# Gate and up side by side for the last 256 feed-forward columns, one group for token numbers and gates, selection sums on TensorE: a diffusion block with expert-choice routing on one core

## The chip, the cores and the metric

The kernel runs on one core of one Trainium2 chip. A core has TensorE (PE in the profile; its weight loads are a line of their own, PEld), VectorE (DVE), ScalarE (ACT), GpSimd (POOL) and SyncE (SP), which here issues most of the transfers. The metric is the time of one execution on the device in microseconds (us); lower is better. The kernel before has a median of 1981.69 us over three runs (1981.35 to 1982.66).

## The reference

One layer over 1024 latent tokens of 1024 numbers and 256 context tokens: a modulated RMSNorm, a token mixer (a Fourier group and a recurrent group), a gated residual, and then the part that this change touches, a mixture of 16 experts in which each expert chooses its 128 tokens. At the end stands a last RMSNorm.

```
def expert_choice_ffn(h, w_router, w_gate, w_up, w_down):
    cap = EC_CAPACITY * n // N_EXPERTS                      # 128 of 1024 tokens
    aff = softmax(h @ w_router)                             # 16 experts
    g, idx = lax.top_k(swapaxes(aff, 1, 2), cap)            # each expert picks its tokens
    xg = h[bidx, idx]
    hid = silu(xg @ w_gate) * (xg @ w_up)                   # 1024 -> 2816 columns
    y = (hid @ w_down) * g[..., None]                       # 2816 -> 1024
    return zeros_like(h).at[bidx, idx].add(y)
```

All of it is float32. An expert has 3 x 1024 x 2816 weights, so the 16 experts read 553.6 MB.

## The kernel before

**The stream of weights.** `make_stream` lists the weights of all experts in halves of 1 MB (128 partitions by 2048 float32). An expert has six groups of hidden columns, five of 512 and a last one of 256. A group of 512 has four gate and up halves (gate, gate, up, up) and two halves of `w_down`; the last group has two halves from one array `wt`, the first with its gate columns and the second with its up columns, and one half of `w_down`. That makes 33 halves an expert, 528 in all. The down halves of a group come behind the gate and up halves of the next one.

**One half.** SyncE loads it into one of ten buffers (`raw`). ScalarE rounds it to the matmul's 32-bit format (`hi`, line 227), VectorE subtracts (`lo`, line 228), into one of four pairs of buffers. TensorE then multiplies three times for each product (`mm3`, line 611): high by high, high by low, low by high. In `moe`, at step m, the order written out by hand is: the matmuls of half m, the activation if a group ended, the rounding of half m + 4, the load of half m + 10, and then whatever `plan` has put at this step. TensorE, ScalarE and VectorE follow this order exactly; a wait of one instruction holds up what is behind it on its engine.

**A group.** `half` (lines 1592 to 1614) puts the gate product of a group into one half of a PSUM tile `gu` and the up product into the other, each in a bank of its own; for the last group the matmuls are 256 columns wide and there are 24 in each half of the stream, for the other groups 512 wide and 12. `act` (line 1616) takes the silu of gate on ScalarE and multiplies by up on VectorE (`hid`). `hid_t` (line 1623) transposes the result on TensorE and splits it again (`hh`, `hl`) for the down product `y`; for the first two experts it stands two steps behind the group's end, for the others one.

**The selection.** In the course of expert 0 and the first half of expert 1, `topk_a`, `topk_p` and `topk_b` find each expert's threshold in 15 rounds, two bits at a time, one round every three steps; each round has six small operations on VectorE and eight matmuls. The first two experts' tokens are already known from the phase before. `gates` (line 1364), at step 3, cuts the routing weights into three bfloat16 parts (`aux`). `topk_end` (line 1399) turns the threshold into slots: masks `m` of the tokens above and at the threshold, for 8 blocks of 128 tokens and 16 experts; the number of such tokens ahead of each token, from a triangular matmul inside a block (line 1410) and from the totals of the blocks (line 1411), which VectorE adds up block by block (`off`, line 1419); then the slot numbers `slT`, partly on VectorE and partly on GpSimd. `plan` puts its four pieces at steps 45, 48, 48 and 49.

**The pick.** `prep` (line 1456) makes a one-hot tile `oh` from the slots on VectorE, multiplies it on TensorE with the token numbers `tokb` (eight matmuls of 2 columns, line 1466) and with the three parts of the gates (eight of 3 columns, line 1468), reduces both on VectorE, and has GpSimd gather the rows. For expert 2 the one-hot tile stands at step 51 and the matmuls at step 54, behind the transposes of expert 1's fourth group.

**Memory.** On the left lie the constants, then a pad of 32 float32 per partition, the ten `raw` buffers and three pairs of `hi` and `lo`; on the right the rest of the expert phase.

Of the kernel before, what the change touches and what calls it, by code (L numbers as in the profile page):

```python
# [99 lines left out]
def lay_out(inp):  # L100
# [22 lines left out]
    for gi, nm in ((0, "lru_wa"), (1, "lru_wi")):  # L123
# [12 lines left out]
        [wg[..., 2560:].transpose(0, 2, 1, 3), wu[..., 2560:].transpose(0, 2, 1, 3)], 2  # L136
# [25 lines left out]
class Kern:  # L162
    HP, HT, LATE = 50, 300, -100
    PAD = 32
# [1199 lines left out]
    def gates(self):  # L1364
        self.aux = self.mo.tile([128, 8, E, 3], BF16, name="aux")
        self.triple(self.aux, self.mo.tile([128, 8, E], F32, name="r1"), self.lg)
# [32 lines left out]
    def topk_end(self):  # L1399
# [9 lines left out]
        mf = m.rearrange("p a b e -> p (a b e)")  # L1409
        nc.tensor.matmul(p[:, 0:256], self.utri, mf, start=True, stop=True)  # L1410
        nc.tensor.matmul(p[:, 256:512], self.ones2, mf, start=True, stop=True)
        yield
        q = S("pre", [2, 8, E])
        V.tensor_copy(q.rearrange("p a b e -> p (a b e)"), p[:, 0:256])
        tot = p[:, 256:512].rearrange("p (a b e) -> p a b e", a=2, b=8)
        off = S("off", [2, 9, E])
        G.memset(off[:, :, 0], 0.0)
        for b in range(8):
            V.tensor_tensor(off[:, :, b + 1], off[:, :, b], tot[:, :, b], op=ALU.add)
        G.tensor_tensor(q, q, off[:, :, 0:8], op=ALU.add)  # L1420
        need = S("need", [E])
        G.tensor_scalar(need, off[:, 0, 8], -1.0, float(CAP), op0=ALU.mult, op1=ALU.add)
        nb = need[:, None].to_broadcast([128, 8, E])
        yield
        sel, sl = S("sel", [8, E]), S("sl", [8, E])
        V.tensor_tensor(sel, q[:, 1], nb, op=ALU.is_lt)
        G.tensor_tensor(sel, sel, m[:, 1], op=ALU.mult)
        G.tensor_tensor(sel, sel, m[:, 0], op=ALU.add)
        V.tensor_tensor(sl, q[:, 1], nb, op=ALU.min)
        G.tensor_tensor(sl, sl, q[:, 0], op=ALU.add)  # L1430
        G.tensor_scalar(sl, sl, 1.0, None, op0=ALU.add)
        self.slT = S("slT", [8, E])
        G.tensor_tensor(self.slT, sl, sel, op=ALU.mult)
# [22 lines left out]
    def prep(self, e):  # L1456
# [8 lines left out]
        for b in range(8):  # L1465
            self.nc.tensor.matmul(p[:, 0:2], oh[:, b], self.tokb[:, b], start=b == 0, stop=b == 7)
        for b in range(8):
            self.nc.tensor.matmul(p[:, 2:5], oh[:, b], self.aux[:, b, e], start=b == 0, stop=b == 7)
# [33 lines left out]
    def make_stream(self):  # L1502
# [3 lines left out]
        def gu(e, j):  # L1506
            self.at[e, j] = len(self.S)
            if j < 5:
                for g, n in ((0, "wg"), (1, "wu")):
                    for h in range(2):  # L1510
                        self.S.append(("g", e, j, g, h, a[n][e, j][:, 2048 * h:2048 * h + 2048]))
            else:
                for g in range(2):
                    self.S.append(("g", e, j, g, 0, a["wt"][e][:, 2048 * g:2048 * g + 2048]))
            self.end[e, j] = len(self.S) - 1
# [76 lines left out]
    def half(self, m):  # L1592
        _, e, j, g, h, _ = self.S[m]
        hi, lo = self.hls.pop(m)
        if self.S[m][0] == "g":
# [4 lines left out]
            w = 512 if j < 5 else 256  # L1600
            nk = 2048 // w
            for i in range(nk):
                k, s = nk * h + i, slice(w * i, w * i + w)
                self.mm3(p[:, g, 0:w], xh[:, k], xl[:, k], hi[:, s], lo[:, s], k == 0, k == KD - 1)
# [11 lines left out]
    def act(self, e, j):  # L1616
        nc = self.nc
        w, p = 512 if j < 5 else 256, self.gu.pop((e, j))
        hid = self.hid[e, j] = self.mo.tile([128, 512], F32, tag="hid", name=f"hid{e}{j}", bufs=2)
        nc.scalar.activation(hid[:, 0:w], p[:, 0, 0:w], AF.Silu)  # L1620
        nc.vector.tensor_tensor(hid[:, 0:w], hid[:, 0:w], p[:, 1, 0:w], op=ALU.mult)  # L1621
# [102 lines left out]
    def plan(self):  # L1724
# [31 lines left out]
        steps((m, m + 3, m + 3, m + 4), tail)  # L1756
        at(m + 4, lambda: next(tail, None))
# [79 lines left out]
```

## Time and profile before

| | |
|---|---|
| median of 3 runs | 1981.69 us (1981.35 to 1982.66) |
| profiled execution | 1983.2 us, its span 1981.4 us |
| busy of the span | TensorE 1899.9 us (96%), VectorE 1750.4 (88%), ScalarE 1357.3 (69%), GpSimd 137.0 (7%) |
| mean granted TensorE clock | 0.980 |
| HBM traffic | 622.98 MB read, 26.74 MB written |
| chain that ended last | TensorE 76%, VectorE 9%, DMA 6% |

The phase before the experts takes the first 430 us; the experts run from there to the end, one each 94.3 us in the regular part. The span runs from the first to the last instruction on the core; the profiled execution's time holds what lies around it too. In a timeline each row is an instruction (or several of one kind, xN): when it started, how long it is shown, and in brackets how long its engine was idle before it and what ended that. A matmul's shown length includes its way through the array, so several overlap; the pace is read from start to start. Notation such as `gu<-hi,xgh` gives the tile written and the tiles read. The granted clock is a share of 2.4 GHz.

### The profile page before, as it was taken

The page shows a single profiled execution, that of the slowest core. Times are in us where ns is not written, and L with a number is a line of the kernel's source. Part 1 is how long each engine was busy: PE and PEld are TensorE (multiplying, and loading weights), DVE is VectorE, ACT ScalarE, POOL GpSimd, SP SyncE. Part 2 cuts the span into 40 slices and gives each one's busy share as a digit, 9 for nine tenths or more (in the row PEclk, how much of TensorE's full clock was granted, in tenths as well). Part 3 has the DMA queues.
Part 4 walks back from the last instruction along what each step waited for, and adds up shares of the span by engine and source line. Part 5 has one row for each costly group of instructions (what it writes and reads, how often), then busy time and mean ns, then how long its engine had stood idle before and what let it go on. Part 6 is the DMA issues. An engine that isn't in the chain of part 4 may idle for free.

```text
span 1981.4 us, 24505 instructions
## 1 busy us (share of the span) xinstructions
PE 1899.9 (96%) x9434; PEld 1559.9 (79%) x9434; DVE 1750.4 (88%) x1629; ACT 1357.3 (69%) x1094; POOL 137.0 (7%) x134
## 2 busy tenths in 40 slices
PE   7989889969999999999999999999999999999996
PEld 2777777857787888888888888888888888888885
DVE  7889787789998989898999999998989898989897
ACT  6567643346676777777777777777777777777775
POOL 2310101220002000000000000000000000000000
PEclk9999989979999999999999999999999999999998
DMA  8353554578999999999999999999999999999994
GB/s 330 112 159 123 191 173 149 207 285 334 350 357 339 379 368 390 381 386 367 388 363 391 355 406 364 396 366 381 379 381 375 384 381 376 385 375 387 366 390 178
DMA packets 113956, 651.34 MB, mean 329 GB/s; under 512 B 12743, under 2 KB 20472, under 8 KB 46254
## 3 DMA queue, kind: packets, MB, share of 16 engines
q1 hardware_dynamic: 100718, 602.55, 79.2%
q0 software_dynamic: 10816, 38.82, 6.9%
q10 hardware_dynamic: 2304, 8.39, 1.1%
q8 instruction: 74, 1.21, 0.2%
q14 instruction: 44, 0.36, 0.0%
HBM read 622.98 MB, written 26.74 MB: 328 GB/s over the span
## 4 chain that ended last, share of the span: by engine, by line
PE 76%; DVE 9%; DMA 6%; issue 5%; ACT 1%; POOL 1%; SPq 0%; POOLq 0%; DVEq 0%; ACTq 0%
PE gu L611 44%; PE y L611 22%; PE mx L611 4%; DVE lo L228 3%; DMA mraw<-in_wmod_dram 3%; PE ht L1627 2%; DMA x<-in_x_dram 1%; DVE macc L839 1%; PE xt L1498 1%; ACT hi L227 1%; DMA trr<-in_trig_dram 1%; PE hp L1185 1%; PE pq L611 1%; DVE g L716 0%; DVE r L714 0%
## 5 line engine op out<-in xcount | busy, mean ns | idle before, releaser
L228 DVE TENSOR_TENSOR lo<-raw,hi 128x2048 fp32r<-128x2048 f32 x525 | 1197.8, 2296 | 130.2 <-ACT hi L227 128.9
L227 ACT ACTIVATE hi<-raw 128x2048 fp32r<-128x2048 f32 x525 | 1006.9, 1918 | 311.2 <-PE gu L611 210.2
L611 PE MATMUL gu<-hi,xgh 128*128 128x512 f32 (+1 forms) x1536 | 580.0, 378 | 0.0
L611 PE MATMUL gu<-hi,xgl 128*128 128x512 f32 (+1 forms) x1536 | 572.9, 373 | 0.0
L611 PE MATMUL gu<-lo,xgh 128*128 128x512 f32 (+1 forms) x1536 | 572.2, 373 | 0.0
L611 PEld LDWEIGHTS gu<-hi,xgl 128*128 128x128 f32 x1536 | 290.2, 189 | 51.8 <-DVE xgl L228 0.2
L611 PEld LDWEIGHTS gu<-lo,xgh 128*128 128x128 f32 x1536 | 290.7, 189 | 49.0 <-issue 0.2
L611 PEld LDWEIGHTS gu<-hi,xgh 128*128 128x128 f32 x1536 | 290.5, 189 | 48.6 <-issue 0.2
L611 PE MATMUL y<-hi,hh 128*128 128x512 f32 x704 | 282.3, 401 | 0.0
L611 PE MATMUL y<-hi,hl 128*128 128x512 f32 x704 | 276.2, 392 | 1.4 <-DVE hl L228 1.4
L611 PE MATMUL y<-lo,hh 128*128 128x512 f32 x704 | 275.0, 391 | 0.0
L611 PEld LDWEIGHTS y<-hi,hl 128*128 128x128 f32 x704 | 132.5, 188 | 30.7 <-DVE hl L228 1.8
L611 PEld LDWEIGHTS y<-lo,hh 128*128 128x128 f32 x704 | 132.9, 189 | 25.5 <-issue 0.2
L611 PEld LDWEIGHTS y<-hi,hh 128*128 128x128 f32 x704 | 132.8, 189 | 25.0 <-issue 0.2
L1620 ACT ACTIVATE hid<-gu 128x512 f32<-128x512 f32 x96 | 54.1, 564 | 87.1 <-PE gu L611 87.1
L1637 POOL DMA_INDIRECT accx<-ys,idx x15 | 24.0, 1598 | 1014.2 <-DVE ys L1636 940.8
L228 DVE TENSOR_TENSOR hl<-ht,hh 128x512 fp32r<-128x512 f32 x96 | 61.4, 640 | 0.0
L1621 DVE TENSOR_TENSOR hid<-hid,gu 128x512 f32<-128x512 f32 x96 | 61.0, 636 | 0.0
L1627 PE MATMUL ht<-k_ident,hid 128*128 128x128 f32 x352 | 54.7, 274 | 5.3 <-DVE hid L1621 5.3
L1627 PEld LDWEIGHTS ht<-k_ident,hid 128*128 128x128 f32 x352 | 44.1, 141 | 19.2 <-DVE hid L1621 7.3
L839 DVE SCALAR_TENSOR_TENSOR macc<-mraw,cond,macc 128x512 f32<-128x512 f32 x56 | 41.8, 748 | 18.8 <-DMA mraw<-in_wmod_dram 18.1
L227 ACT ACTIVATE hh<-ht 128x512 fp32r<-128x512 f32 x96 | 52.0, 542 | 3.5 <-PE ht L1627 3.5
(434 smaller groups left out, 1819.6 us busy)
## 6 DMA issues: line engine op xcount, KB each, us to landing
raw<-in_wg_dram SPq DMA_DIRECT2D x160, 1024.0 KB, 7.1
raw<-in_wu_dram SPq DMA_DIRECT2D x160, 1024.0 KB, 7.3
raw<-in_wd_dram SPq DMA_DIRECT2D x160, 1024.0 KB, 7.1
raw<-in_wt_dram SPq DMA_DIRECT2D x32, 1024.0 KB, 7.7
mraw<-in_wmod_dram POOLq DMA_DIRECT2D x32, 512.0 KB, 4.7
raw<-in_wdt_dram SPq DMA_DIRECT2D x16, 1024.0 KB, 6.9
wm<-in_wmod_dram SPq DMA_DIRECT2D x16, 512.0 KB, 9.7
wr<-in_win_dram SPq DMA_DIRECT2D x24, 256.0 KB, 3.5
```

What stands on the lines that cost most here:

```text
L227: i = self.nc.scalar.activation(hi, src, AF.Copy)
L228: j = (eng or self.nc.vector).tensor_tensor(lo, src, hi, op=ALU.subtract)
L611: i = nc.tensor.matmul(out, l, r, start=st, stop=sp)
L839: nc.vector.scalar_tensor_tensor(acc, w[:, i], c, acc, op0=ALU.mult, op1=ALU.add)
L1185: self.pin(nc.tensor.matmul(q[:, 1024:1024 + E], hT[:, k], wr[:, k], start=k == 0, stop=k == KD - 1))
L1498: nc.tensor.transpose(p[:, 128 * i:128 * i + 128], xg[:, 128 * k:128 * k + 128], self.ident)
L1620: nc.scalar.activation(hid[:, 0:w], p[:, 0, 0:w], AF.Silu)
L1621: nc.vector.tensor_tensor(hid[:, 0:w], hid[:, 0:w], p[:, 1, 0:w], op=ALU.mult)
L1627: self.nc.tensor.transpose(q[:, c:c + 128], hid[:, c:c + 128], self.ident)
L1637: self.nc.gpsimd.indirect_dma_start(out=self.accx, out_offset=bass.IndirectOffsetOnAxis(ap=idx[:, :1], axis=0), in_=ys, in_offset=None, co ...
```

## The change

The array `wt` is laid out anew: for each of the eight blocks of 128 input rows the 256 gate columns stand beside the 256 up columns, so a half of the stream holds four blocks with gate and up. `half` then runs 12 matmuls of 512 columns for these halves as for all others, into one PSUM bank; `act` reads up from columns 256 to 511 of it. `aux` gets two more columns, into which VectorE copies the token numbers once for all experts; the pick is one group of eight matmuls with 5 columns. In `topk_end` TensorE adds the totals: seven matmuls add each block's total to all later blocks in the PSUM of the triangular product, and eight of 16 columns sum up the tokens above the threshold. The copy, the eight running sums and GpSimd's operations go; what is left runs on VectorE, in one piece at step 49, behind the matmuls at step 48. The pad grows to 64.

```diff
     out["wt"] = np.stack(
-        [wg[..., 2560:].transpose(0, 2, 1, 3), wu[..., 2560:].transpose(0, 2, 1, 3)], 2
+        [wg[..., 2560:].transpose(0, 2, 1, 3), wu[..., 2560:].transpose(0, 2, 1, 3)], 3
     ).reshape(E, 128, 4096)
...
-    PAD = 32
+    PAD = 64
...
     def gates(self):
-        self.aux = self.mo.tile([128, 8, E, 3], BF16, name="aux")
-        self.triple(self.aux, self.mo.tile([128, 8, E], F32, name="r1"), self.lg)
+        self.aux = self.mo.tile([128, 8, E, 5], BF16, name="aux")
+        self.triple(self.aux[..., 2:5], self.mo.tile([128, 8, E], F32, name="r1"), self.lg)
+        self.nc.vector.tensor_copy(self.aux[..., 0:2], self.tokb[:, :, None, :].to_broadcast([128, 8, E, 2]))
...
+        pre = p[:, 0:256].rearrange("p (a b e) -> p a b e", a=2, b=8)
         nc.tensor.matmul(p[:, 0:256], self.utri, mf, start=True, stop=True)
-        nc.tensor.matmul(p[:, 256:512], self.ones2, mf, start=True, stop=True)
+        for b in range(7):
+            nc.tensor.matmul(pre[:, :, b + 1:8], self.ones2, m[:, :, b, None, :].to_broadcast([128, 2, 7 - b, E]),
+                             start=False, stop=True, skip_group_check=True)
+        for b in range(8):
+            nc.tensor.matmul(p[:, 256:256 + E], self.ones2, m[:, 0, b], start=False, stop=b == 7, skip_group_check=True)
         yield
-        q = S("pre", [2, 8, E])
-        V.tensor_copy(q.rearrange("p a b e -> p (a b e)"), p[:, 0:256])
-        tot = p[:, 256:512].rearrange("p (a b e) -> p a b e", a=2, b=8)
-        off = S("off", [2, 9, E])
-        G.memset(off[:, :, 0], 0.0)
-        for b in range(8):
-            V.tensor_tensor(off[:, :, b + 1], off[:, :, b], tot[:, :, b], op=ALU.add)
-        G.tensor_tensor(q, q, off[:, :, 0:8], op=ALU.add)
         need = S("need", [E])
-        G.tensor_scalar(need, off[:, 0, 8], -1.0, float(CAP), op0=ALU.mult, op1=ALU.add)
+        V.tensor_scalar(need, p[:, 256:256 + E], -1.0, float(CAP), op0=ALU.mult, op1=ALU.add)
         nb = need[:, None].to_broadcast([128, 8, E])
-        yield
         sel, sl = S("sel", [8, E]), S("sl", [8, E])
-        V.tensor_tensor(sel, q[:, 1], nb, op=ALU.is_lt)
-        G.tensor_tensor(sel, sel, m[:, 1], op=ALU.mult)
-        G.tensor_tensor(sel, sel, m[:, 0], op=ALU.add)
-        V.tensor_tensor(sl, q[:, 1], nb, op=ALU.min)
-        G.tensor_tensor(sl, sl, q[:, 0], op=ALU.add)
-        G.tensor_scalar(sl, sl, 1.0, None, op0=ALU.add)
         self.slT = S("slT", [8, E])
-        G.tensor_tensor(self.slT, sl, sel, op=ALU.mult)
+        V.tensor_tensor(sel, pre[:, 1], nb, op=ALU.is_lt)
+        V.tensor_tensor(sl, pre[:, 1], nb, op=ALU.min)
+        V.tensor_tensor(sl, sl, pre[:, 0], op=ALU.add)
+        V.tensor_tensor(sel, sel, m[:, 1], op=ALU.mult)
+        V.tensor_tensor(sel, sel, m[:, 0], op=ALU.add)
+        V.scalar_tensor_tensor(self.slT, sl, 1.0, sel, op0=ALU.add, op1=ALU.mult)
...
         for b in range(8):
-            self.nc.tensor.matmul(p[:, 0:2], oh[:, b], self.tokb[:, b], start=b == 0, stop=b == 7)
-        for b in range(8):
-            self.nc.tensor.matmul(p[:, 2:5], oh[:, b], self.aux[:, b, e], start=b == 0, stop=b == 7)
+            self.nc.tensor.matmul(p[:, 0:5], oh[:, b], self.aux[:, b, e], start=b == 0, stop=b == 7)
...
-                for g in range(2):
-                    self.S.append(("g", e, j, g, 0, a["wt"][e][:, 2048 * g:2048 * g + 2048]))
+                for h in range(2):
+                    self.S.append(("g", e, j, 0, h, a["wt"][e][:, 2048 * h:2048 * h + 2048]))
...
-            w = 512 if j < 5 else 256
-            nk = 2048 // w
-            for i in range(nk):
-                k, s = nk * h + i, slice(w * i, w * i + w)
-                self.mm3(p[:, g, 0:w], xh[:, k], xl[:, k], hi[:, s], lo[:, s], k == 0, k == KD - 1)
+            for i in range(4):
+                k, s = 4 * h + i, slice(512 * i, 512 * i + 512)
+                self.mm3(p[:, g], xh[:, k], xl[:, k], hi[:, s], lo[:, s], k == 0, k == KD - 1)
...
+        up = p[:, 1] if j < 5 else p[:, 0, 256:512]
         nc.scalar.activation(hid[:, 0:w], p[:, 0, 0:w], AF.Silu)
-        nc.vector.tensor_tensor(hid[:, 0:w], hid[:, 0:w], p[:, 1, 0:w], op=ALU.mult)
+        nc.vector.tensor_tensor(hid[:, 0:w], hid[:, 0:w], up, op=ALU.mult)
...
-        steps((m, m + 3, m + 3, m + 4), tail)
-        at(m + 4, lambda: next(tail, None))
+        steps((m, m + 3, m + 4), tail)
```

## Rows read from the trace of the kernel before

**Rows 1.** Stretches: start:end, length, busy per engine (instructions), granted clock, DMA, GB/s
```profile
435.00:535.00 100.00, 94.30 (x522) 76.25 (x521) 98.28 (x111) 66.73 (x47) 9.21 (x4) 1.00 0.91 340
603.00:614.00 11.00, 8.19 (x40) 6.40 (x39) 9.61 (x9) 3.10 (x4) 1.85 (x3) 0.69 0.79 300
1000.00:1200.00 200.00, 200.00 (x1008) 168.12 (x1008) 181.11 (x110) 147.84 (x101) 5.18 (x4) 1.00 0.98 378
```
**Rows 2.** Waits of TensorE from 480 us on: us in total, times, longest
```profile
PE ht L1627 <- DVE hid L1621: 5.3, 3, 2.8
```
**Rows 3.** Waits of ScalarE and of VectorE from 480 us on
```profile
ACT hi L227 <- PE gu L611: 204.3, 242, 5.1
...
DVE lo L228 <- ACT hi L227: 128.9, 336, 1.5
```
**Rows 4.** Timeline of TensorE, the last 256 columns of one expert
```profile
1005.49 0.28 PE L611 MATMUL gu<-hi,xgh 128*128 128x256 f32 x1
...
1011.25 0.40 PE L611 MATMUL y<-hi,hh 128*128 128x512 f32 x1
```
**Rows 5.** Timeline of TensorE, one half of 512 columns
```profile
595.70 0.39 PE L611 MATMUL gu<-hi,xgh 128*128 128x512 f32 x1
...
598.42 0.39 PE L611 MATMUL y<-hi,hh 128*128 128x512 f32 x1
```
**Rows 6.** Timeline of VectorE, end of its full stretch
```profile
535.95 2.29 DVE L228 TENSOR_TENSOR lo<-raw,hi 128x2048 fp32r<-128x2048 f32 x1 [0.50 <-ACT hi L227]
```
**Rows 7.** Timeline of TensorE, the last transposes
```profile
1957.74 0.44 PE L1627 MATMUL ht<-k_ident,hid 128*128 128x128 f32 x2 [2.31 <-DVE hid L1621]
```
**Rows 8.** Timeline of TensorE, the pick of expert 3
```profile
678.92 0.35 PE L1466 MATMUL px<-tokb,oh 128*128 128x2 bf16 x8
...
679.34 0.48 PE L611 MATMUL gu<-hi,xgh 128*128 128x512 f32 x1
```
**Rows 9.** Timeline of VectorE, a cast of the gates
```profile
455.30 0.28 DVE L1486 CAST aux<-r 128x128 bf16<-128x128 f32 x1
```
**Rows 10.** Timelines of VectorE and ScalarE, the end of the selection
```profile
593.07 0.42 DVE L1414 COPY pre<-tcf 128x256 f32<-128x256 f32 x1
593.18 1.92 ACT L227 ACTIVATE hi<-raw 128x2048 fp32r<-128x2048 f32 x1 [0.80 <-PE gu L611]
595.05 2.29 DVE L228 TENSOR_TENSOR lo<-raw,hi 128x2048 fp32r<-128x2048 f32 x1
598.14 0.29 DVE L1426 TENSOR_TENSOR sel<-pre,need 128x128 f32<-128x128 f32 x1 [0.81 <-POOL need L1422]
598.56 5.02 DVE L228 TENSOR_TENSOR lo<-raw,hi 128x2048 fp32r<-128x2048 f32 x2
604.96 1.23 DVE L1461 TENSOR_TENSOR oh<-k_iota,slT 128x1024 bf16<-128x1024 f32 x1 [1.39 <-POOL slT L1433]
606.11 0.68 DVE L1621 TENSOR_TENSOR hid<-hid,gu 128x512 f32<-128x512 f32 x1
```
**Rows 11.** Timeline of TensorE around its longest wait
```profile
586.87 0.60 PE L1627 MATMUL ht<-k_ident,hid 128*128 128x128 f32 x4
...
603.65 0.39 PE L611 MATMUL y<-hi,hl 128*128 128x512 f32 x1
606.84 1.11 PE L1627 MATMUL ht<-k_ident,hid 128*128 128x128 f32 x4 [2.81 <-DVE hid L1621]
...
613.47 0.40 PE L611 MATMUL gu<-hi,xgh 128*128 128x512 f32 x1
```
**Rows 12.** Timeline of TensorE, the selection sums
```profile
587.30 0.27 PE L1410 MATMUL tcf<-m,k_utri 128*128 128x256 bf16 x1
587.41 0.27 PE L1411 MATMUL tcf<-m,ones 128*128 128x256 bf16 x1
```
**Rows 13.** SyncE's waits and its loads' landing from 1000 to 1200 us
```profile
SPq L1580 <- DVE lo L228: 157.8, 64, 3.6
...
DMA to landing us min/median/max: 5.9/7.2/9.3
```

## The prediction

> **What bounds the kernel now.** I read the table of stretches first. From 1000 to 1200 us TensorE is busy for all of the 200 us at a granted clock of 1.00, VectorE for 181 and ScalarE for 148 [rows 1]. A full bar alone doesn't make TensorE the bound, so the waits come next: in the whole expert phase from 480 us TensorE waits for another engine only at three kinds of place, and the large one is the transposes of the hidden values behind VectorE, 5.3 us in three waits, the longest 2.8 [rows 2]. The others wait for TensorE: ScalarE's rounding of the weights waits 204.3 us for the gate and up matmuls that free its buffers, and VectorE waits 128.9 us for ScalarE [rows 3]. So in the regular experts the end moves with every nanosecond of TensorE, and VectorE, the next engine, has about a tenth of its time free.
>
> Two stretches differ. From 435 to 535 us VectorE is busy for 98.3 of 100 us [rows 1]: the first expert shares it with the token selection, and there time on VectorE counts, and time on TensorE doesn't. The second is one wait near 604 us, where the selection ends; the timeline around it carries the largest term below.
>
> **Part 1, the last 256 columns.** Before, gate and up of an expert's last 256 columns are 48 matmuls of 256 columns; they start at 1005.49 and the next product at 1011.25, so 5.76 us [rows 4], 0.120 each. After, 24 matmuls of 512. Twelve of those take 595.70 to 598.42, 2.72 us, 0.227 each [rows 5], so 24 take 5.44. The halves don't add up because a start-to-start time of 0.227 for 512 columns and 0.120 for 256 is 0.107 per 256 columns and about 13 ns per matmul, and 24 of these 13 ns go. That is 0.32 us an expert; a few 512-column steps are longer than 0.227, so I take 0.30 (0.24 to 0.36). Experts 0 to 14 count: their tails lie after VectorE has caught up, which it has at 535.95, where it waits for ScalarE again [rows 6]; expert 0's tail, just before, also runs on TensorE's time. In expert 15 it is lost, as the transposes behind it wait 2.31 us for VectorE anyway [rows 7]. 15 x 0.30 = 4.5 us. Rounding, loads and the later multiplication keep count and shape; the wait for both halves was there already.
> The Trainium skill has a fixed cost per back-to-back matmul too, but about 2.5 ns once the clock is up (TensorE: Matmul & The Clock Gate, section "Wait — 56ns, not 53.3ns?"). By that this part would bring 24 x 2.5 ns x 15 = 0.9 us and not 4.5, an estimate from that page; the steps of this trace say 13 ns.
>
> **Part 2, token numbers and gates in one group.** Sixteen matmuls of 2 and 3 columns take 678.92 to 679.34, 0.42 us [rows 8], some 26 ns each; eight of 5 columns then take 0.21. Their width can't matter much: the steps of 2 and of 3 columns are alike. The pick of expert 1 falls in VectorE's stretch and doesn't count, those of experts 2 to 15 do: 14 x 0.21 = 2.9 us (2.5 to 3.1). The two reductions on VectorE stay.
> Its price is the copy of the token numbers beside the gates, 128x256, once, in VectorE's full stretch. One of the three casts there, 128x128, takes 0.28 us [rows 9] and a copy of 128x256 out of PSUM 0.42 [rows 10]. I take 0.3 lost (0 to 0.5): nothing hides it, since VectorE has no idle time there.
>
> **Part 3, selection sums on TensorE.** Here is the wait. At 603.65 TensorE issues the last product before a transpose; the transposes start at 606.84, 3.19 us later where a step is 0.23. They wait for VectorE's hidden values of expert 1, group 3. After this idle time the clock is at 1.2 GHz for some us: the granted clock averages 0.69 over 603 to 614 [rows 1]. From 603.65 to 613.47, where the steps are short again, 9.82 us pass [rows 11]. The same work at 2.4 GHz is 0.23 (step) + 0.43 (four transposes, 586.87 to 587.30) + 0.42 (the pick) + 2.81 (twelve matmuls, with the 0.09 that the first one after a pick takes longer) = 3.89. So the wait costs 5.9 us, half of it as clock.
>
> Why is VectorE late? Its last stretch before the hidden values, which it starts at 606.11, holds [rows 10]: the copy and the eight running sums, 593.07 to 595.05 = 1.98 us; a wait for GpSimd of 0.81; two comparisons, 598.14 to 598.56 = 0.42; two weight splits that take 5.02 beside GpSimd's work, where the one before takes 2.29, so 0.4 more; and a wait for GpSimd of 1.39 ahead of the one-hot tile. Together 5.0 us. After: seven small operations in a row, at about 0.21 each (the two comparisons' step), 1.5 us, perhaps 2.0 since several read PSUM. So the hidden values are ready 3.0 to 3.5 us earlier, at about 603.3 to 603.8 instead of 606.8. Their inputs allow it: ScalarE rounds one half of the weights each 2.7 us, the second of the three in question by 595.1 [rows 10], and VectorE would come to it at 596.8. TensorE wants the hidden values at 603.9, and later still by what it now adds. That leaves a margin of 0.5 to 1.1 us. The 5.9 us go, and what is late next is TensorE itself.
>
> What TensorE adds: one product of 256 columns as before, seven of 224 down to 32 columns (896 in all), eight of 16. 256 columns of this type take 0.11 [rows 12], so 896 take 0.39 by columns and 0.77 if each costs a whole 0.11; eight small ones 0.2. Sum 0.7 to 1.1 against 0.22 for the two that go: 0.5 net (0.45 to 0.9), on the path. The new wait is VectorE's for these sums; they are issued a whole half (2.7 us) before VectorE comes to them, so it is empty. Behind VectorE's block stand the splits for the next halves, needed 3 us later and more. GpSimd's seven operations go and free nobody else; its gather of expert 2's rows only starts earlier. The PSUM tile of the sums is held a little longer; its buffer is next wanted five halves later.
>
> **Sum.** 4.5 + 2.9 + 5.9 - 0.3 - 0.5 = 12.5 us. It is made against the profiled execution (1983.2 us, span 1981.4), which is 1.5 over the median; all its terms are differences, so I take them off the median: 1981.7 - 12.5 = 1969.2 us. The likeliest case by itself spans 1966.5 to 1971.5.
>
> **Rivals.** (a) VectorE is still late at 604 us. For: the margin is 1 us, and the seven operations are chained and partly read PSUM; from 2.5 to 3 us in all on, the wait is back. Against: their like takes 0.21. Price: 1.5 us if short, all 5.9 if the clock falls again, so 1971 to 1975.2.
> (b) The loads set the pace. For: the DMA engines are 98% busy at 378 GB/s from 1000 to 1200 [rows 1], and the same bytes must now come in less time. Against: a load is issued when VectorE frees its buffer, SyncE waiting 157.8 us for that in these 200 us, and lands 7.2 us (at most 9.3) later [rows 13], while ten buffers of about 2.8 us each mean that it is read some 20 us after its issue. Even with no faster loads, 12 us would be eaten from that reserve over the whole run. If it holds nevertheless, parts 1 and 2 are lost: 12.5 - 7.4 = 5.1, 1976.6 us.
> The Trainium skill gives about 358 GB/s as a core's HBM limit (DMA: Bandwidth & Descriptors, section "Where 436 GB/s comes from"), by which case (b) would rule already; the 378 GB/s of the trace speak against it as a limit.
> (c) Merging two matmuls saves little because the 13 ns are no cost per matmul; part 1 brings 1 us: 1972.7. Against it stand the 512-column rows themselves.
> (d) Slower: the pad and the wider tile move every weight buffer by 128 bytes and the right-hand tiles by more. All 6336 weight matmuls of 512 columns (528 halves of 12) read there while three others write. A step longer by 2 ns eats the gain; 4 ns would give 1969.2 + 25 = 1994. No row shows dependence on the place; the buffers' neighbours stay the same.
>
> **How the numbers follow.** The forecast has 0.70, (a) 0.13, (b) 0.07, (c) 0.05, (d) 0.05. The range from 1966.5 to 1975 holds the forecast's spread, (c) and most of (a), and leaves out (b) and (d), what is left of (a), and a little of the forecast's own edge. A run can tell 0.2%, 4 us, from no change: faster is the forecast, (a), (c) and most of (b), 0.91; no change 0.05 (the rest of (b), small forms of (d)); slower 0.04.
>
> **What would show it.** Right: no 256-column gate and up matmuls, and 5.4 us for each expert's tail block; eight matmuls in 0.2 us at each pick; no wait of the transposes near 604 us and a granted clock of 1.00 from 603 to 614; experts 93.75 us apart instead of 94.27. Wrong: that wait still there with VectorE's block over 2.5 us (a); ScalarE waiting for loads of weights (b); tail blocks of 5.7 us (c); 512-column steps over 0.229 on the average (d).

## The result, and the profile after

| | before | after |
|---|---|---|
| median of 7 runs each | 1981.65 us (1977.43 to 1985.10) | 1970.58 us (1966.70 to 1973.56) |
| profiled execution, its span | 1983.2 us, 1981.4 us | 1968.55 us, 1966.7 us |
| mean granted TensorE clock | 0.980 | 0.985 |

The ratio of after to before is 0.9946 [0.9932, 0.9961], so the kernel is 11.1 us faster by the medians (7.7 to 13.5 by the interval); 12.5 were forecast. Runs of one kernel lie some 4 us to either side of their median. In the profiled executions the part ahead of the experts is what differs: the first gate and up matmul starts between 430.2 and 436.5 us in the fourteen profiles of this study. The distances between experts repeat to a few hundredths of a us, so the steps are measured there. What does not repeat is the stretch behind expert 15's last transposes, 22.3 to 23.7 us (without the two kernels that change this end), the longer where the clock falls behind the wait there; it is 23.7 in both profiles compared here. From the first gate and up matmul to the end it is 1548.68 us before and 1535.65 after, 13.0 us less.

The table of stretches of the kernel after, in the columns of [rows 1]:
```profile
435.00:535.00 100.00, 93.69 (x488) 74.11 (x489) 98.03 (x112) 66.93 (x46) 6.19 (x4) 1.00 0.92 339
603.00:614.00 11.00, 11.00 (x59) 9.21 (x58) 10.58 (x8) 8.16 (x5) 2.86 (x1) 1.00 0.97 357
1000.00:1200.00 200.00, 200.00 (x927) 165.07 (x926) 181.52 (x110) 148.69 (x101) 5.15 (x4) 1.00 1.00 383
```
From 603 to 614 us TensorE is now busy for all of 11 us at a granted clock of 1.00, where [rows 1] has 8.19 us at 0.69. From 1000 to 1200 us it has 927 matmuls for 1008 in the same full 200 us. VectorE's first stretch is as full as it was.

TensorE's waits from 470 us on in the kernel after, to be read against [rows 2]:
```profile
PE ht L1620 <- DVE hid L1614: 3.0, 2, 2.7
```
The longest is now the wait at the end of expert 15, the one of [rows 7]; the wait near 604 us is gone. The others still wait for TensorE and ScalarE as in [rows 3], from 480 us on in the kernel after:
```profile
ACT hi L227 <- PE gu L611: 198.8, 242, 1.9
```
```profile
DVE lo L228 <- ACT hi L227: 119.7, 336, 0.6
```
The place of the lost wait in the timeline of TensorE, kernel after, against [rows 11]:
```profile
602.72 0.39 PE L611 MATMUL y<-hi,hl 128*128 128x512 f32 x1
602.95 0.60 PE L1620 MATMUL ht<-k_ident,hid 128*128 128x128 f32 x4
603.38 0.34 PE L1462 MATMUL px<-aux,oh 128*128 128x5 bf16 x8
603.59 0.47 PE L611 MATMUL gu<-hi,xgh 128*128 128x512 f32 x1
...
606.42 0.39 PE L611 MATMUL gu<-hi,xgh 128*128 128x512 f32 x1
```
The same stretch, from the last product before the transposes to the thirteenth matmul behind the pick, took 603.65 to 613.47 = 9.82 us; it now takes 602.72 to 606.42 = 3.70. The pick in it is eight matmuls in 0.21 us, where [rows 8] has sixteen in 0.42.

Why the wait went is in VectorE's timeline of the kernel after, against [rows 10]:
```profile
593.75 0.16 DVE L1420 TENSOR_SCALAR need<-tcf 128x16 f32<-128x16 f32 x1
593.95 0.29 DVE L1424 TENSOR_TENSOR sel<-tcf,need 128x128 f32<-128x128 f32 x1
...
595.32 0.29 DVE L1429 SCALAR_TENSOR_TENSOR slT<-sl,sel 128x128 f32<-128x128 f32 x1
595.53 4.49 DVE L228 TENSOR_TENSOR lo<-raw,hi 128x2048 fp32r<-128x2048 f32 x2
599.94 1.22 DVE L1457 TENSOR_TENSOR oh<-k_iota,slT 128x1024 bf16<-128x1024 f32 x1
601.07 0.68 DVE L1614 TENSOR_TENSOR hid<-hid,gu 128x512 f32<-128x512 f32 x1
```
The seven operations take 593.75 to 595.53, 1.78 us. No bracket stands in the block: nothing in it waits for GpSimd. The hidden values are ready at 601.07 + 0.68 = 601.75; TensorE comes to them at 602.95, 1.2 us later.

The price on TensorE, the sums of the kernel after, against [rows 12]:
```profile
585.39 0.60 PE L1620 MATMUL ht<-k_ident,hid 128*128 128x128 f32 x4
585.82 0.27 PE L1412 MATMUL tcf<-m,k_utri 128*128 128x256 bf16 x1
585.93 0.55 PE L1414 MATMUL tcf<-m,ones 128*128 128x224 bf16 x7
586.33 0.35 PE L1417 MATMUL tcf<-m,ones 128*128 128x16 bf16 x8
586.53 0.48 PE L611 MATMUL gu<-hi,xgh 128*128 128x512 f32 x1
```
Before, the next matmul behind the two of [rows 12] is
```profile
587.44 0.48 PE L611 MATMUL gu<-hi,xgh 128*128 128x512 f32 x1
```
From 585.82 to 586.53 are 0.71 us for sixteen matmuls; the two of before took 587.30 to 587.44, 0.14, so 0.57 is added.

A tail block of the kernel after, against [rows 4]: the first of its 24 matmuls, and the next product.
```profile
996.22 0.39 PE L611 MATMUL gu<-hi,xgh 128*128 128x512 f32 x1
...
1001.66 0.39 PE L611 MATMUL y<-hi,hh 128*128 128x512 f32 x1
```
5.44 us for 5.76, and the same within 0.01 in each of experts 2 to 14. From one expert's last transposes to the next one's it is 93.71 us on the average (experts 3 to 14; 93.68 to 93.72) for 94.27.

### The profile page after: what moved, and what is told of

The parts are those of the page before. It is cut to its first block, busy times and chain, and to the rows that moved or that the text cites. A ratio compares the mean times of both kernels' runs of the same rounds, so it can differ in the third digit from the quotient of the medians.

```text
span 1966.7 us, 23514 instructions
## 1 busy us (share of the span) xinstructions
PE 1883.7 (96%) x8944; PEld 1530.9 (78%) x8944; DVE 1749.7 (89%) x1626; ACT 1357.4 (69%) x1094; POOL 126.6 (6%) x126
## 3 DMA queue, kind: packets, MB, share of 16 engines
q8 instruction: 70, 1.15, 0.2%
## 4 chain that ended last, share of the span: by engine, by line
PE 79%; DVE 8%; DMA 6%; issue 5%; ACT 1%; POOL 0%; SPq 0%; POOLq 0%; DVEq 0%; ACTq 0%
PE gu L611 46%; PE y L611 23%; PE mx L611 4%; DMA mraw<-in_wmod_dram 3%; DVE lo L228 3%; PE ht L1620 2%; DMA wm<-in_wmod_dram 1%; DVE macc L839 1%; PE xt L1492 1%; DMA trr<-in_trig_dram 1%; PE hp L1185 1%; PE pq L611 1%; ACT hi L227 1%; DVE g L716 0%; DVE r L714 0%
## 5 line engine op out<-in xcount | busy, mean ns | idle before, releaser
L611 PE MATMUL gu<-hi,xgh 128*128 128x512 f32 x1408 | 556.2, 395 | 0.0
L611 PE MATMUL gu<-lo,xgh 128*128 128x512 f32 x1408 | 548.7, 390 | 1.4 <-DVE lo L228 1.4
L611 PE MATMUL gu<-hi,xgl 128*128 128x512 f32 x1408 | 548.9, 390 | 0.0
L611 PEld LDWEIGHTS gu<-hi,xgl 128*128 128x128 f32 x1408 | 264.4, 188 | 56.4 <-DVE xgl L228 0.2
L611 PEld LDWEIGHTS gu<-lo,xgh 128*128 128x128 f32 x1408 | 264.8, 188 | 55.7 <-DVE lo L228 1.8
L611 PEld LDWEIGHTS gu<-hi,xgh 128*128 128x128 f32 x1408 | 264.6, 188 | 52.7 <-issue 0.2
```

The costliest lines, as they stand in the source:

```text
L611: i = nc.tensor.matmul(out, l, r, start=st, stop=sp)
```

## The experiments

Each ratio is to the kernel before, run on the same chip in the same rounds. Two landmarks recur: the *distance* from one expert's last transposes to the next one's in the regular part, and the *late stretch*, from the transposes of expert 1's third group over those of the fourth to those of the fifth (19.97 + 20.24 us before, 17.56 + 17.08 after).

**The three parts alone.** Each was put on the kernel before by itself: the layout of `wt` with `half` and `act`; `gates` with the pick; `topk_end` with `plan` and the pad.
```diff
-[wg[..., 2560:].transpose(0, 2, 1, 3), wu[..., 2560:].transpose(0, 2, 1, 3)], 2
+[wg[..., 2560:].transpose(0, 2, 1, 3), wu[..., 2560:].transpose(0, 2, 1, 3)], 3
...
```


> Only part 1: the kernel before, with the last 256 columns of gate and up side by side in 512-column matmuls. Theory (a matmul costs TensorE about 13 ns beside its columns): the distance from one expert's last transposes to the next goes from 94.27 us to about 93.95; the wait near 604 us stays as it was, 2.8 us of waiting and the slow clock behind it, and eats expert 0's share; the whole is 14 x 0.3 = 4.2 us less than before, some 1977.4. Rival (c) (the 13 ns are no cost per matmul): the distance is 94.2, the whole 1 us less. Rival (b) (loads set the pace): distance 94.27, no change.


Measured: median 1977.73 us for 1980.26, ratio 0.9985 [0.9976, 0.9995]. The distance is 93.89 to 93.94, 0.35 us less than before. The tail block by itself is 0.31 us shorter, which is 13.0 ns for each of the twenty-four matmuls that went; the other 0.04 lies in the steps outside the block, and no run here tells why. The wait near 604 us stays (2.77 us), but the slow clock behind it is shorter: 0.84 from 603 to 614 us.
```diff
-            self.nc.tensor.matmul(p[:, 0:2], oh[:, b], self.tokb[:, b], start=b == 0, stop=b == 7)
-        for b in range(8):
-            self.nc.tensor.matmul(p[:, 2:5], oh[:, b], self.aux[:, b, e], start=b == 0, stop=b == 7)
+            self.nc.tensor.matmul(p[:, 0:5], oh[:, b], self.aux[:, b, e], start=b == 0, stop=b == 7)
...
```


> Only part 2: the kernel before, with the token numbers copied beside the gates and one group of eight 5-column matmuls for each pick. Theory: the distance from expert to expert goes from 94.27 to about 94.05 us (eight steps of 26 ns less); the first expert gets 0.4 us longer through the copy on VectorE (the changed kernel showed 14.99 against 14.58 us between its first two groups of transposes); the whole is 14 x 0.21 - 0.4 = 2.5 us less than before, 1979.1. Rival (b): distance 94.27, and only the 0.4 us are left, slower.


Measured: 1978.81 us, 0.9991 [0.9980, 1.0001], which by itself shows no gain. The landmarks do: the distance is 94.07, 0.20 less, and the copy makes expert 0's second group 0.39 us later (14.58 to 14.96). The wait near 604 us stays here too, and this time no slow clock follows it: TensorE's stretch from 603 to 614 us, first in the part 1 kernel,
```profile
603.00:614.00 11.00, 8.22 (x46) 6.41 (x45) 9.62 (x7) 4.43 (x3) 3.77 (x4) 0.84 0.76 270
```
and then in the part 2 kernel,
```profile
603.00:614.00 11.00, 8.24 (x46) 6.59 (x45) 9.62 (x6) 5.64 (x4) 2.74 (x3) 1.00 0.79 286
```
shows the same idle time, 2.8 us of 11, at granted clocks of 0.84 and 1.00. So the wait itself is 2.8 us in all three kernels, and what the clock adds behind it is not the same from one to the next.
```diff
-            V.tensor_tensor(off[:, :, b + 1], off[:, :, b], tot[:, :, b], op=ALU.add)
-        G.tensor_tensor(q, q, off[:, :, 0:8], op=ALU.add)
+            nc.tensor.matmul(p[:, 256:256 + E], self.ones2, m[:, 0, b], start=False, stop=b == 7, skip_group_check=True)
...
-    PAD = 32
+    PAD = 64
```


> Only part 3: the kernel before, with the selection sums on TensorE, the rest of them on VectorE, none on GpSimd. Theory: the wait near 604 us and the slow clock behind it are gone; from the transposes of expert 1's third group to those of its fifth it takes about 34.8 us instead of 40.21; the distance between later experts stays 94.27; the whole is 5.4 us less than before, 1976.2. Rival (a) in its weaker form (the wait goes only because all three parts together leave VectorE room): a wait of 0.5 us or more is left here and the gain is under 4 us.


Measured: 1975.35 us, 0.9976 [0.9966, 0.9986]. The late stretch is 17.62 + 17.26 = 34.88 us for 40.21, without a wait, at a granted clock of 1.00; the distance is 94.24, nearly as before. From 603 to 614 us in this kernel:
```profile
603.00:614.00 11.00, 11.00 (x49) 9.11 (x49) 10.39 (x8) 7.35 (x5) 2.86 (x1) 1.00 0.96 348
```
So the part on the selection alone removes the wait, and no smaller wait follows it. Rival (a) falls.

**The buffers' place.** The kernel after, with the pad of before.
```diff
-    PAD = 64
+    PAD = 32
```


> The changed kernel with the pad at 32 as before, so that all weight buffers on the left lie 128 bytes lower and no longer at the same address modulo 256 as those on the right. Theory (the place of the buffers costs nothing): as the changed kernel, 1970.6 within 2 us, distance between experts 93.71. Rival (d) (steps depend on the place): the mean step of the 512-column matmuls, 227.4 ns in the changed kernel, moves by 1 ns or more and the distance by 0.4 us or more; a smaller shift of 0.05 to 0.1 us in the distance would say that the part of the gain that was over the forecast (0.565 us an expert instead of 0.51) is from the place.


Measured: 1998.08 us (1996.43 to 1999.74), 1.0085 [1.0070, 1.0099]: 128 bytes on the left side of the memory cost 27.5 us against the kernel after (25.0 us over the expert phase in the profiles) and turn the gain into a loss. The distance is 95.3 to 95.5. The groups of lines from 1000 to 1200 us (busy us, mean ns of one, idle before), kernel after,
```profile
L611 PE MATMUL gu<-hi,xgh 128*128 128x512 f32 x187 | 73.6, 393 | 0.0
L611 PE MATMUL gu<-hi,xgl 128*128 128x512 f32 x187 | 72.9, 390 | 0.0
L611 PE MATMUL gu<-lo,xgh 128*128 128x512 f32 x187 | 72.8, 389 | 0.0
```
and with the pad of 32:
```profile
L611 PE MATMUL gu<-hi,xgh 128*128 128x512 f32 x181 | 72.0, 398 | 0.0
L611 PE MATMUL gu<-hi,xgl 128*128 128x512 f32 x182 | 71.7, 394 | 0.0
L611 PE MATMUL gu<-lo,xgh 128*128 128x512 f32 x181 | 71.2, 394 | 0.0
```
No idle time in either, five or six matmuls fewer of each kind in the same 200 us: the single matmul is longer. The timeline of TensorE with the pad of 32 tells which:
```profile
1050.19 0.39 PE L611 MATMUL y<-lo,hh 128*128 128x512 f32 x1
...
1052.70 0.40 PE L611 MATMUL gu<-hi,xgh 128*128 128x512 f32 x1
...
1055.50 0.40 PE L611 MATMUL gu<-hi,xgh 128*128 128x512 f32 x1
...
1058.30 0.40 PE L611 MATMUL gu<-hi,xgh 128*128 128x512 f32 x1
```
The halves from 1052.70 and 1055.50 take 2.80 us for 12 matmuls, 233 ns each; the half before, 11 matmuls from 1050.19, takes 2.51, 228 each. Its weights lie in the fourth pair of `hi` and `lo`, on the right, where the token tiles lie too; the three slow pairs lie on the left. Over all steps from 680 to 1920 us, without the first one behind a transpose or a pick, the means are 232.5 to 233.2 ns for the left pairs and 228.5 to 228.6 for the right one; in the kernels before and after all four have 227.1 to 227.7. By the program's addresses both sides begin alike modulo 256 bytes before (at 160 and 160) and after (32 and 32), since parts 2 and 3 move the right side by 1664 bytes and the pad the left by 128. With the pad of 32 it is 160 and 32. The parts run alone keep the sides alike, part 2 with the pad of 32 (160 and 160) and part 3 with its own of 64 (32 and 32).

Two more pads test that reading, both on the kernel after: one that keeps the sides alike modulo 256 at another address, and one that makes them differ by 64 bytes.
```diff
-    PAD = 64
+    PAD = 128
```


> The changed kernel with a pad of 128 instead of 64, so that all buffers on the left lie 256 bytes higher. The run with pad 32 had steps of 231.9 ns in place of 227.4, in the halves whose weights lie on the left (232.8) and hardly in those whose weights lie on the right beside the other operand (228.5). Theory E (what counts is whether left and right lie alike modulo 256): steps of 227.4 again, distance 93.71, 1970.6 us. Rival F (the place itself counts, 64 is just a good one): steps off 227.4 by 1 ns or more, the whole 6 us or more off.


Measured: 1970.13 us, 0.9956 [0.9944, 0.9968], the distance 93.67 to 93.71, the mean step 227.4 ns as in the kernel after. A row of this kernel, from 1000 to 1200 us as above:
```profile
L611 PE MATMUL gu<-hi,xgh 128*128 128x512 f32 x187 | 73.6, 393 | 0.0
```
Alike is fast at all the addresses tried.
```diff
-    PAD = 64
+    PAD = 48
```


> The changed kernel with a pad of 48, so that left and right differ by 64 bytes modulo 256 (0 with pads of 64 and 128, 128 with a pad of 32). Theory E1 (the step grows evenly with the distance): steps of some 229.6 ns, distance between experts 94.5, the whole 13 us over the changed kernel. E2 (any difference is as bad as 128 bytes): 231.9 ns and 28 us. E3 (only 128 bytes are bad): 227.4 ns and no change.


Measured: 1996.03 us (1995.17 to 1999.36), 1.0086 [1.0070, 1.0102]; the distance 95.56 to 95.61, left pairs 233.3 ns, the right one 228.8. The same row here:
```profile
L611 PE MATMUL gu<-hi,xgh 128*128 128x512 f32 x181 | 72.0, 398 | 0.0
```
A difference of 64 bytes costs as much as one of 128. Why is not settled; other differences were not tried, and the 1 ns that the right pair loses is not explained.

**What a matmul costs beside its columns.** The kernel after with the fifth group of each expert in 256-column matmuls, 48 more an expert for the same columns.
```diff
+                if j == 4:
+                    for l, q, last in ((xh, hi, False), (xh, lo, False), (xl, hi, True)):
+                        for c in range(2):
+                            self.nc.tensor.matmul(p[:, g, 256 * c:256 * c + 256], l[:, k], ...
```


> The changed kernel with the fifth group of every expert (512 columns of gate and up) in matmuls of 256 columns, two for one: 96 instead of 48 an expert, same columns, same weights. Theory (about 13 ns for each matmul beside its columns): 48 x 13 ns = 0.62 us an expert, distance 93.71 to 94.33, the whole 9 to 10 us more than the changed kernel, about 1980. Rival (c): with 2.5 ns a matmul as the Trainium skill has it (TensorE: Matmul & The Clock Gate) it would be 0.12 us an expert and 1.9 us in all.


Measured: 1978.19 us, 0.9996 [0.9987, 1.0006] (before here: 1980.19). The distance is 94.30, 0.59 to 0.60 us more than after, so 12.4 ns for each added matmul. In the timeline of this kernel, TensorE, rows of two matmuls:
```profile
991.03 0.40 PE L1599 MATMUL gu<-lo,xgh 128*128 128x256 f32 x2
...
993.66 0.40 PE L611 MATMUL y<-hi,hh 128*128 128x512 f32 x1
```
22 matmuls in 2.63 us are 0.1195 each, 0.239 a pair where a 512-column one takes 0.227. So a matmul has a cost of its own beside its columns, and case (c) does not hold.

**GpSimd alone?** The kernel before with GpSimd's arithmetic of `topk_end` on VectorE, and TensorE as it was.
```diff
-        G.tensor_tensor(q, q, off[:, :, 0:8], op=ALU.add)
+        V.tensor_tensor(q, q, off[:, :, 0:8], op=ALU.add)
...
-        G.tensor_tensor(self.slT, sl, sel, op=ALU.mult)
+        V.tensor_tensor(self.slT, sl, sel, op=ALU.mult)
```


> The kernel before, with GpSimd's operations at the end of the selection moved to VectorE as they are; the copy and the eight running sums stay, no sums on TensorE. Theory (the wait near 604 us is the sum of VectorE's own work and its waits for GpSimd): VectorE's block is about 4.2 us instead of 5.0 with waits, so the wait of the transposes goes from 2.8 to about 2 us and the slow clock behind it stays; the whole 1 us less than before, up to 3. Rival (GpSimd alone is the cause): the wait is gone and the whole 5.9 us less than before.


Measured: 1981.72 us, 1.0011 [0.9999, 1.0023]. TensorE's waits from 470 us on in this kernel:
```profile
PE ht L1627 <- DVE hid L1621: 3.7, 3, 2.3
PE xt L1498 <- DMA xg<-hxd,idx: 2.0, 1, 2.0
...
PE y L611 <- DVE lo L228: 0.4, 1, 0.4
```
and in its timeline the transposes in question:
```profile
605.28 0.66 PE L1627 MATMUL ht<-k_ident,hid 128*128 128x128 f32 x4 [1.15 <-DVE hid L1621]
```
The wait shrinks from 2.81 to 1.15 us, with 0.4 us for a weight split ahead of it, and no slow clock follows (the second half of the late stretch is 17.36). But a new wait comes: the gather of expert 2's rows lands 2.0 us late, the granted clock falls behind it (0.89 from 625 to 640 us), and the step from the fifth group's transposes to the last ones' is 16.23 us for 12.53. So the gain at the wait is given back, and the expected gain of 1 us did not come. The rival did not hold either: waiting for GpSimd was not all of VectorE's lateness. The gather starts only behind VectorE's index reductions, at 612.77 us, and these stand behind three weight splits that follow the hidden values. The kernel after has neither wait, since VectorE's block is 1.78 us for what takes 4.3 here (592.45 to 599.01 without the split between).

**More bytes.** The kernel after, 28 of the halves loaded twice into their buffers, 5% more bytes.
```diff
-            self.nc.sync.dma_start(self.raws[m], self.S[m][5])
+            for _ in range(2 if m % 16 == 15 and 60 < m < 500 else 1):
+                self.nc.sync.dma_start(self.raws[m], self.S[m][5])
```


> The changed kernel with 28 of the 528 halves of weights loaded twice into the same buffer (each sixteenth half from the 63rd on), 5% more bytes at the same pace of work; 382 GB/s would have to become 406. Theory (the loads have room and ten buffers of reserve): no change, 1970.6 within 2 us, distance 93.71. Rival (b) (the loads are at their limit): the reserve of some 20 us is used up by half of the run, then the distance grows towards 99 us; the whole 30 to 55 us more.


Measured: 1970.75 us, 0.9958 [0.9945, 0.9971]; the distance is 93.71 as without. The stretch from 1000 to 1200 us:
```profile
1000.00:1200.00 200.00, 200.00 (x926) 165.13 (x925) 181.63 (x111) 148.48 (x101) 5.15 (x4) 1.00 1.01 405
```
405 GB/s for 383, and TensorE as full as without. Rival (b) falls: a DMA share near 1.00 in these rows is no limit by itself.

**Two things that were left.** First the copy, the one term that costs: the gates and the copy on GpSimd, the kernel after otherwise.
```diff
-        self.triple(self.aux[..., 2:5], self.mo.tile([128, 8, E], F32, name="r1"), self.lg)
-        self.nc.vector.tensor_copy(self.aux...
+        self.triple(self.aux[..., 2:5], self.mo.tile([128, 8, E], F32, name="r1"), self.lg, self.nc.gpsimd)
+        self.nc.gpsimd.tensor_copy(self.aux...
```


> The changed kernel with the cutting of the gates and the copy of the token numbers (six operations at step 3) on GpSimd instead of VectorE. Theory (in the first expert VectorE is the bound, so what leaves it is gained): from the first transposes to the second 13.3 us instead of 14.99, 13.8 if GpSimd's work beside it slows VectorE's splits; the whole 1.2 to 1.7 us less than the changed kernel. Rival: GpSimd is so slow beside VectorE that the gates are late for the pick of expert 1; the time is as before or longer.


Measured: 1968.90 us, 0.9946 [0.9933, 0.9959]. From the first to the second group's transposes of expert 0 it is 13.17 us for 14.99, but up to the first 20.50 for 19.99: 1.3 us less, which whole runs don't tell from the kernel after (0.9946 to 0.9958 for it and its like). The 0.5 us come from GpSimd's work beside VectorE's. VectorE in this kernel,
```profile
445.91 2.39 DVE L1381 TENSOR_TENSOR cand<-k_pats,T 128x48 int32<-128x48 int32 x1
```
and GpSimd beside it:
```profile
441.62 2.49 POOL L1480 CAST aux<-r 128x128 bf16<-128x128 f32 x1
443.87 4.36 POOL L1709 TENSOR_TENSOR accg<-accg,bg 1x1024 f32<-1x1024 f32 x1
```
Here GpSimd's addition is moved behind the casts, and VectorE's small operation ends as it ends, at 448.3; in the kernel after that operation is 0.19 us long. But there the addition runs beside two weight splits and stretches these:
```profile
437.79 6.68 DVE L228 TENSOR_TENSOR lo<-raw,hi 128x2048 fp32r<-128x2048 f32 x2
```
```profile
437.49 2.62 POOL L1709 TENSOR_TENSOR accg<-accg,bg 1x1024 f32<-1x1024 f32 x1
```
Two splits take 4.49 elsewhere. So the addition costs VectorE some 2 us in either kernel, at another place. With the casts beside the splits in addition, VectorE reaches the operation behind the small one 14.03 us after the first gate and up matmul for 13.53.

Then the wait at the end, which part 1 could not use. The order of the last scalings and roots is written so that none of them stands before expert 15's hidden values; `p0`, which loads ScalarE's table for the roots early, is left out. In this order the write of the last row block no longer stands behind the writes of the token tiles, so output rows of expert 15's tokens are overwritten: the edit shows what the order costs and is no version to use.
```diff
-    FIN = {..., 8: "q6", 6: "q7 r08 n08 s0", 5: "s1",
-           4: "p0 s2 s3", 3: "s4 s5", 2: "s6", 1: "y8 s7 r81 n81 s8 w8"}
+    FIN = {..., 8: "q6", 6: "q7",
+           3: "r08 n08 s0 s1", 1: "y8 s2 r81 n81 s8 w8 s3 s4 s5 s6 s7"}
```


> The changed kernel with the order of the last norm changed: the roots of the first eight token tiles, their Newton step and the scaling come behind the last expert's last hidden values instead of before them, so ScalarE doesn't change its table twice ahead of these. Theory (the wait of 2.7 us before the last transposes, which also ate expert 15's share, is the queue of ScalarE and VectorE): the wait is gone, with it the slow clock behind it, the last product ends 4 to 5 us earlier, and the end is 3 to 4 us earlier, about 1967. Rival (what is moved back comes last): the eight scalings, 1.2 us each, end behind the last row's write; the end is as late as before or later.


Measured: 1970.57 us, 0.9955 [0.9942, 0.9968]. The end of the kernel after, TensorE and GpSimd:
```profile
1943.06 0.44 PE L1620 MATMUL ht<-k_ident,hid 128*128 128x128 f32 x2 [2.66 <-DVE hid L1614]
...
1950.18 0.39 PE L611 MATMUL y<-hi,hl 128*128 128x512 f32 x1
...
1959.18 0.97 POOL L1689 DMA_INDIRECT out_dram<-ysL,idx  x1 [77.67 <-DMA out_dram<-fin]
```
and of this kernel, with VectorE's last scalings:
```profile
1941.34 0.38 PE L1620 MATMUL ht<-k_ident,hid 128*128 128x128 f32 x2
...
1946.80 0.39 PE L611 MATMUL y<-hi,hl 128*128 128x512 f32 x1
...
1954.18 6.06 DVE L1683 SCALAR_TENSOR_TENSOR fin<-fin,rsf,fgb 128x1024 f32<-128x1024 f32 x5
```
The wait is gone and the last product starts 7.1 us behind the transposes after, 5.5 here, so TensorE ends 4.4 us earlier counted from expert 14. Only 2.8 of that is the wait: most of the rest is the slow clock behind it, which the profile of the kernel after has and the one with the gates on GpSimd has not (there the last product starts 5.5 us behind the transposes too). But five scalings now stand behind the last rows, 1954.18 to 1960.24, and their stores behind them: from the last product to the end it is 21.90 us for 16.56. The gain at the wait is given back by the stores.

Both edits together:


> The changed kernel with both: gates on GpSimd and the roots behind the last hidden values. If each works by itself they add up, since one lies in the first expert and the other at the end: 1965 to 1966 us, 0.992 of the kernel before. If one of them costs time by itself, the sum of the two.


Measured: 1970.47 us, 0.9954 [0.9942, 0.9966]. The end repeats that of the late roots (21.90 us). Up to the first transposes it is 22.01 us and from there to the second group's 11.69, together 33.70 as with the gates alone (20.50 + 13.17); the granted clock is 0.89 from 440 to 455 us here and 1.00 there. So the two edits do not add up to a gain, and the rows of expert 15 are overwritten here too. No version here beats the kernel after by what runs can tell.

## Why the prediction was right

Taken over the whole expert phase the account is: 0.41 more for the copy, 0.27 less for expert 0's tail, 5.74 less for expert 1, 7.40 less for experts 2 to 14 (13 times 0.57), nothing for expert 15. That is the 13.0 us of the profiles, for a forecast of 12.5. By its steps:

- **The bound.** TensorE sets the distance between experts, to within a few hundredths of a us: each part's saving on it appears in full, and 5% more load traffic not at all. Three views, the stretches, TensorE's own waits and what the other engines wait for [rows 1 to 3], were enough to say so.
- **Part 1**, 0.30 an expert by the steps of [rows 4, 5]: alone it measured 0.35, inside the range given, of which the block itself is 0.31. The Trainium skill (TensorE: Matmul & The Clock Gate, section "Wait — 56ns, not 53.3ns?") has about 2.5 ns of fixed cost per matmul. The 13.0 ns of the block and the 12.4 of the split group, both at a granted clock of 1.00, speak against that figure for these 32-bit matmuls, each with a weight load of its own. Expert 15's tail was saved and eaten by the wait behind it, as forecast: 2.66 us for 2.31 [rows 7].
- **Part 2**, 0.21 a pick from [rows 8]: 0.20. Both together, 7.4 in the forecast, come to 8.1 in the kernel after, about 5.0 and 2.8 by the parts alone; the rest, 0.03 an expert, appears with part 3 (94.24 us), in steps that are a little shorter on the average (227.6 ns before, 227.5 with part 3 alone, 227.4 after); why is not shown.
- **The copy**, 0.3 (0 to 0.5): 0.41 on TensorE's time. VectorE's block from the first cast to the next round's first operation is 1.75 us for 1.42, and not by the copy alone: a cast into the wider tile takes 0.35 us for the 0.28 of [rows 9].
- **The wait at 604 us**, 5.9: 9.82 - 3.70, less the 0.21 of the pick, is 5.91 in these two profiles. VectorE's block, put at 1.5 to 2.0 us, took 1.78, and the margin, given as 0.5 to 1.1 us, is 1.2. The part that was less certain than the working shows is the clock's. Half of the 5.9 us was its share, and the kernels with part 1 or part 2 alone have the same wait with less slow clock or none behind it. That the whole runs gain 11.1 and not 13.0 us (some 10 by the medians for the pad of 128 and the double loads, which have the same steps) fits a before whose other runs have less of it, but no run here shows how often; it stays open.
- **The new sums**, 0.5 (0.45 to 0.9): 0.57. The seven take 0.40 for 896 columns, so they cost by columns, as the lower bound had it; the eight small ones 0.20. What the working had too high is what goes: 0.22 for the two of before, which took 0.14.
- **The rivals.** (a), (b) and (c) were refuted by runs of their own. On (b), the Trainium skill gives about 358 GB/s as the HBM limit of a core, half of the 716 of a stack with two cores (DMA: Bandwidth & Descriptors, section "Where 436 GB/s comes from"). This kernel, on one core, carried 405 over 200 us at no cost, so the measurement decides. (d) is the one whose weight was wrong. "No row shows dependence on the place" was true of the trace, and the price worked out, 4 ns a step and 25 us, is nearly what the pad of 32 costs: 4.5 ns and 27.5 us. The change escapes it because its new pad restores the likeness of the two sides that the rest of the change breaks. Nothing in the working knew of that, so that (d) did not come true was luck for the forecast. The 0.05 was a guess on a place that the addresses in the program could have narrowed. The rows shown [rows 1 to 13] hold nothing on it, and a pad in a tuned kernel's diff was read as a neutral shift.

The study's own expectations failed in four places. The pad of 32 was to cost nothing and cost 27.5 us. VectorE taking GpSimd's work was to bring some gain, and the gather took it; the gates on GpSimd cost 0.5 us at a place nobody had looked at, and the late roots moved the end from TensorE to the stores. In the last three the wait or the work named was shortened, and the next in the row decided.

## What to carry to other kernels

Where one engine is full and the others wait for it, a change's worth is its count of instructions on that engine by the start-to-start steps of the trace; matmuls of half the width cost a fixed sum each, here 12 to 13 ns. A single wait costs more than its length when the clock falls behind it, but that share differs from kernel to kernel, so it belongs in the range and not in the sum. Any edit that moves buffers, a pad, a tile grown or dropped, can be an edit to every matmul's step: compare the addresses of its operands before and after, and read the mean step first.

## What the runs showed of the hardware

- The step of a 512-column matmul depends on how the buffers of its two operands lie to each other: 227.4 ns where both sides of the memory begin alike modulo 256 bytes (pads 64 and 128), 232.5 to 233.4 where they differ by 128 or 64 bytes (pads 32 and 48), with no idle time of TensorE in the stretch. In the same two kernels the pair that lies beside its other operand has 228.5 to 228.9. The Trainium skill (SBUF — State Buffer, section "SBUF: two separate sides") has TensorE never wait on anyone at its ports. The trace shows no wait either, but longer steps; what lengthens them no run here tells, so the rows decide neither for the page nor against it.
- A 128x48 operation on VectorE took 2.39 us in place of 0.19 beside an addition on GpSimd, and ended as that ended. In the kernel after the same addition ran beside two weight splits, which took 6.68 us for the 4.49 of two others. The same section of the Trainium skill has the two engines share a pair of ports that one of them holds for a whole instruction. These rows agree.
- The same idle time of TensorE, 2.8 us near 604 us, was followed by a granted clock of 0.69, 0.84 or 1.00 over 603 to 614 us in three kernels (before, part 1 alone, part 2 alone).
